# Hybrid attention and retention trunk on one core: lower parts of V, queries and keys deferred by a tick, retention's norm a round later, norms and output scales one operation per round

## The chip, the core and the metric

The kernel runs on one core of a Trainium2 chip. A core has five engines with instruction queues of their own: TensorE (PE) does matmuls into PSUM, VectorE (DVE), ScalarE (ACT) and GpSimd (POOL) do elementwise work, and SyncE (SP) issues nearly all DMA transfers of this kernel. Each engine works through its queue in order, and waits at an instruction whose inputs or buffers are not ready. The metric is the time of one execution on the device in microseconds. The kernel before takes 2124.11 us, the median of 3 runs (2123.64 to 2125.86).

## What is computed

A trunk of two layers over 2048 tokens of width 1024. Each layer normalizes its input, projects it to eight sections of 512 columns, sends four through chunked attention (8 heads of 64) and three through chunkwise retention (4 heads of 128) with gates for both, and projects back with a residual. Cut to what matters:

```python
def hybrid_layer(x, norm_gain, w_in, w_out, rel_bias, cos, sin):
    hn = rms_norm(x, norm_gain)
    aq, ak, av, ag, rq, rk, rv, rg = jnp.split(hn @ w_in, cuts, axis=-1)
    ya = chunked_rel_attention(aq, ak, av, rel_bias)      # own chunk of 64 and 8 before
    yr = chunkwise_retention(rq, rk, rv, cos, sin)        # rotary q and k, decayed state, rms_norm per head
    y = jnp.concatenate([ya * jax.nn.silu(ag), yr * jax.nn.silu(rg)], axis=-1)
    return x + y @ w_out

def reference(x, positions, norm_gain, w_in, w_out, rel_bias, final_gain):
    cos, sin = rotary_tables(positions, RET_HEAD_DIM)
    for layer in range(DEPTH):
        x = hybrid_layer(x, ...)
    return rms_norm(x, final_gain)
```

Inputs and output are f32. The kernel computes each f32 product as three f16 products: each operand is held as an upper f16 part and a lower part (what the upper leaves over), and high x high, high x low and low x high are summed in PSUM.

## The kernel before

**Tiles and stages.** The tokens are 16 tiles of 128, four of them a block n (0 to 3). The columns are worked off in four groups s (0 to 3), of two attention heads and one retention head. A *stage* is (layer l, group s, block n): `dense_T` makes q, k and the two rotary sections, transposed (four groups of 24 matmuls with 512 columns), `dense_V` makes the attention's v, retention's v and both gates (four tiles, 24 matmuls each), and `attention` with `retention` inside works through the block's eight units of (tile, head) and four retention tiles. The attention of a stage runs one dense generator later, beside the next stage's matmuls. After the four groups, `wout` multiplies the gated output y with w_out, adds the residual and makes the next layer's normalized input (`residual`) or the output (`final`).

**What sets the order.** Everything is written as Python generators that `run` (L1113) interleaves. A round is: one step of the dense generator (a third, 8 matmuls); then `tick` (L613); then one step of the attention generator; then `pull` of some background steps (weight preparation, input norms, rotary tables), so many that the pushed steps are used up in the rounds left. The order of emission is the order in each engine's queue.

```python
def later(k, fn):
    deferred.append([k, fn])          # run by the k-th tick from now

def run(gen, att, thirds):
    for _ in gen:
        tick()
        ... next(att[0], att) ...
        ... pull(min(-(-todo // max(left, 1)), todo)) ...
```

A `later(1, ...)` made in a dense step is therefore run by the tick of the same round, after the older deferred steps that are due in it; one made in an attention or a background step is run in the next round.

**Evacuation of PSUM.** In `dense_T`, `evacuate` copies q (L637) and k (L647) to f16 on ACT; DVE takes the lower part from the same PSUM buffer and the copy (L638, L648), and SP spreads the halves over partitions. The rotary sections are copied to `raw`, swapped by DMA, turned with the tables by POOL (L668 to L670) and split (L673, L676, L679). In `dense_V` ACT makes the upper part of v, the gate's tanh and the upper part of retention's v (L757 to L759), and DVE makes the lower parts and the gate (L760, L762, L764).

**Retention.** For each tile, r1 holds the scores; three deferred steps mask them (L867), make dT's upper (L852) and lower part (L856). r2, from the same PSUM pool `psR` of four buffers (shared with the attention's output o and with the sums ms of weight preparation), holds the output in its first 128 columns and the state's increment in the next. Deferred steps follow: at 1 the state is added up (L888) and ACT squares the output into the SBUF tile `yr` (L909, one buffer) with a sum per row; at 2 the new state's upper part (L852) and the root (DVE L901, POOL L902); at 3 its lower part (L856) and the scaled, gated output (DVE L905), stored to `y_d` by SP (L907); at 4 the state is decayed (ACT L896).

**Norms and tables in the background.** Blocks 1, 2 and 3 need their input norms while group 0 runs: `norm` squares a tile with a row sum (ACT L206), takes the root (DVE L210, POOL L212), multiplies by root and gain (DVE L229), splits into halves (ACT L242, DVE L243) and transposes them by SP DMA into hTh and hTl (L250, L251). `norms_from_input` (L1127) interleaves the tiles of a block; block 1's are the list of steps at L1301, and blocks 2 and 3 are pushed at L1325 with 21 steps, followed by the rotary `tables` of the next block (DVE L93 to L124, stores L129 to L132) with 19 steps.

**Output projection.** `wout` (L1032) runs 6 rounds per tile. For the tile two ahead it loads y, squares it and scales (`y_scale`: ACT L938, DVE), splits it a round later (`y_split`: ACT L245, DVE L246), and turns it by SP transposes (`y_turn`) in round 0. The residual sum is L1069; `residual` then puts the next layer's norm steps at 2 to 8 rounds on, `final` the output's.

Of the kernel before, what the change touches and what calls it, by code (L numbers as in the profile page):

```python
# [18 lines left out]
P = 128  # L19
# [8 lines left out]
def hybrid_trunk(ctx: ExitStack, tc: tile.TileContext, x, pos, gain, gcol, w_in, w_out, rel, fgain,  # L28
# [174 lines left out]
    def rms(xt, m, e, nm, junk):  # L203

        ss = b2.tile([P, 1], F32, tag="ss", name=f"ss{nm}", bufs=4)
        act.activation(junk, xt, AF.Square, accum_out=ss)  # L206
        return rms_of(ss, m, e, nm)

    def rms_of(ss, m, e, nm):
        dve.tensor_scalar(ss, ss, m, e, op0=ALU.mult, op1=ALU.add)  # L210
# [10 lines left out]
    def norm(l, t, xt, rows=None):  # L221

        n, a = divmod(t, 4)
        hT_of(l, n)
        hh, hl = (h_[:, :, a * P:(a + 1) * P] for h_ in hT[l, n])
        nm = f"n{l}_{t}"
        rs = rms(xt.rearrange("p (k c) -> p k c", c=P), gains[l].m, gains[l].e, nm, hh)
        yield
        dve.scalar_tensor_tensor(out=xt, in0=xt, scalar=rs[:, 0:1], in1=gains[l].b, op0=ALU.mult, op1=ALU.mult)  # L229
        yield  # L230
        rw = split_rows(xt, nm, rows)
        yield
        transpose_rows(rw, hh, hl)
        yield

    def split_rows(xt, nm, rows=None, s_=None):

        if rows is None:
            rows = (b2.tile([P, 1280], F16, tag="sc", name=f"rh{nm}")[:, 0:D],
                    b2.tile([P, 1280], F16, tag="pq", name=f"rl{nm}")[:, 0:D])  # L240
        if s_ is None:
            act.activation(rows[0], xt, AF.Copy)  # L242
            dve.tensor_tensor(rows[1], xt, rows[0], op=ALU.subtract)  # L243
        else:
            act.activation(rows[0], xt, AF.Copy, scale=s_[:, 0:1])  # L245
            dve.scalar_tensor_tensor(out=rows[1], in0=xt, scalar=s_[:, 0:1], in1=rows[0], op0=ALU.mult, op1=ALU.subtract)  # L246
        return rows
# [374 lines left out]
    def dense_T(l, s, n, g, st):  # L622
# [9 lines left out]

        def evacuate(j, ps):
            if j == 0:
# [3 lines left out]
                dve.scalar_tensor_tensor(out=qq[:, 1, :], in0=ps, scalar=2.0 ** -16, in1=qq[:, 0, :], op0=ALU.mult,  # L638
                                         op1=ALU.subtract)
                for hx in range(2):  # L640
                    for half in range(2):
                        sp.dma_start(st.q[half * 64:half * 64 + 64, hx], qq[hx * 64:hx * 64 + 64])
            elif j == 1:
# [4 lines left out]
                dve.scalar_tensor_tensor(out=kl, in0=ps, scalar=2.0 ** -16, in1=kh, op0=ALU.mult, op1=ALU.subtract)  # L648
                sp.dma_start(st.k[0:64, 0, :], kh[0:64, :])
# [294 lines left out]
    def y_split(u):  # L944
        split_rows(u.y, u.nm, u.rows, u.sy)
# [496 lines left out]
```

## Time and profile before

| | us |
|---|---|
| median of 3 runs | 2124.11 |
| range of the runs | 2123.64 to 2125.86 |
| the profiled execution | 2123.54 |
| its span in the profile | 2121.8 |
| PE busy | 2018.0 (95%), 14014 matmuls |
| DVE busy | 1217.7 (57%) |
| ACT busy | 1161.2 (55%) |
| POOL busy | 687.7 (32%) |
| mean granted TensorE clock | 0.986 |

The page gives shares and slices of the span and the costliest groups of instructions. A group's row names line, engine, operation and tiles, then its busy time, the mean of one in ns, and the idle time before it with what ended it. Rows of waits read: engine, line that waited, what released it; then microseconds in total, times, and the longest. Rows of windows read: stretch and its length, then the busy time (and count) of PE, PEld (weight load), DVE, ACT and POOL, then the granted clock as a share of full speed, the busy share of the 16 DMA engines, and GB/s. Rows of a timeline read: start, duration, engine, line, operation, out<-in; in brackets the idle time before, with its releaser.

The execution falls into a prologue with stage (0,0,0) (0 to 75 us), the other stages of layer 0 (to 902), the first output projection (to 1102), the stages of layer 1 (to 1933) and the second output projection.

### The profile page before, as it was taken

The page shows a single profiled execution, that of the slowest core. Times are in us where ns is not written, and L with a number is a line of the kernel's source. Part 1 is how long each engine was busy: PE and PEld are TensorE (multiplying, and loading weights), DVE is VectorE, ACT ScalarE, POOL GpSimd, SP SyncE. Part 2 cuts the span into 40 slices and gives each one's busy share as a digit, 9 for nine tenths or more (in the row PEclk, how much of TensorE's full clock was granted, in tenths as well). Part 3 has the DMA queues.
Part 4 walks back from the last instruction along what each step waited for, and adds up shares of the span by engine and source line. Part 5 has one row for each costly group of instructions (what it writes and reads, how often), then busy time and mean ns, then how long its engine had stood idle before and what let it go on. Part 6 is the DMA issues. An engine that isn't in the chain of part 4 may idle for free. (4 is left out here: it accounts for less than half of the span.)

```text
span 2121.8 us, 39588 instructions
## 1 busy us (share of the span) xinstructions
PE 2018.0 (95%) x14014; PEld 1054.6 (50%) x14014; DVE 1217.7 (57%) x3839; ACT 1161.2 (55%) x2522; POOL 687.7 (32%) x701
## 2 busy tenths in 40 slices
PE   6788999999999999988999999999999999999998
PEld 4344455554455555444444555555545545554443
DVE  7677656555655555566653556555655565556543
ACT  7455665556655654555444546555665565556432
POOL 1233343443334334421002443434334433343200
PEclk9999999999999999999999999999999999999999
DMA  8757774558655764689865556555685566548874
GB/s 246 177 118 148 153 161 106 112 110 185 152 115 110 160 157 101 134 185 246 232 176 116 120 104 141 121 127 101 142 192 122 100 142 159 123 103 177 213 204 119
DMA packets 645702, 313.64 MB, mean 148 GB/s; under 512 B 459232, under 2 KB 602080, under 8 KB 645504
## 3 DMA queue, kind: packets, MB, share of 16 engines
q1 hardware_dynamic: 645504, 311.12, 65.4%
q8 instruction: 109, 1.79, 0.3%
q14 instruction: 89, 0.73, 0.1%
HBM read 123.26 MB, written 41.98 MB: 78 GB/s over the span
## 5 line engine op out<-in xcount | busy, mean ns | idle before, releaser
L803 POOL TENSOR_TENSOR pq<-sc,pq 128x640 f16<-128x640 f32 (+4 forms) x256 | 319.5, 1248 | 1037.1 <-ACT pq L802 622.9
L800 ACT ACTIVATE sc<-sc,mq,cT 128x640 f32<-128x640 f32 (+4 forms) x256 | 218.3, 853 | 359.6 <-DVE mq L799 241.6
L749 PE MATMUL dV<-wlV,hTh 128*128 128x512 f16 x1024 | 391.9, 383 | 5.4 <-DVE wlV L347 5.4
L749 PE MATMUL dV<-whV,hTh 128*128 128x512 f16 x1024 | 392.1, 383 | 4.6 <-DVE gt L764 3.7
L749 PE MATMUL dV<-whV,hTl 128*128 128x512 f16 x1024 | 391.8, 383 | 0.0
L729 PE MATMUL dT<-hTh,whT 128*128 128x512 f16 x1008 | 383.9, 381 | 6.2 <-DMA hTh<-hTl 6.2
L729 PE MATMUL dT<-hTl,whT 128*128 128x512 f16 x1008 | 383.5, 380 | 3.0 <-DMA hTl<-hTl 3.0
L729 PE MATMUL dT<-hTh,wlT 128*128 128x512 f16 x1008 | 383.5, 380 | 0.0
L749 PEld LDWEIGHTS <-hTh 128*128 128x128 f16 x2048 | 199.3, 99 | 224.8 <-issue 9.0
L729 PEld LDWEIGHTS <-whT 128*128 128x128 f16 x2016 | 194.9, 98 | 225.7 <-issue 11.5
L797 DVE CUSTOM_DVE_ANT_0 sc<-S,bias 128x640 f32<-128x640 f32 (+4 forms) x256 | 188.7, 737 | 145.6 <-PE S L794 144.7
L1066 PE MATMUL dO<-whO,yhy 128*128 128x512 f16 x512 | 194.7, 380 | 2.2 <-DVE hTl L1069 1.2
L1066 PE MATMUL dO<-whO,yly 128*128 128x512 f16 x512 | 194.7, 380 | 2.2 <-DMA yly<-rly 2.2
L1066 PE MATMUL dO<-wlO,yhy 128*128 128x512 f16 x512 | 194.8, 380 | 0.0
L802 ACT ACTIVATE pq<-sc 128x640 f16<-128x640 f32 (+4 forms) x256 | 171.5, 670 | 8.1
L760 DVE SCALAR_TENSOR_TENSOR v<-dV,v 128x128 f16<-128x128 f32 x128 | 37.2, 291 | 214.1 <-ACT rv L759 213.2
L749 PEld LDWEIGHTS <-hTl 128*128 128x128 f16 x1024 | 100.8, 98 | 116.3 <-issue 11.4
L1066 PEld LDWEIGHTS <-yhy 128*128 128x128 f16 x1024 | 99.9, 98 | 117.9 <-issue 4.7
L729 PEld LDWEIGHTS <-wlT 128*128 128x128 f16 x1008 | 98.9, 98 | 105.2 <-issue 2.3
L793 PE MATMUL S<-k,q 128*128 128x128 f16 (+3 forms) x592 | 143.4, 268 | 7.3 <-DVE mq L797 4.4
L813 PE MATMUL o<-v,pT 128*128 128x65 f16 x1120 | 130.6, 194 | 12.5 <-DMA pT<-pq 12.5
L814 PE MATMUL o<-v,pT 128*128 128x64 f16 x1120 | 130.8, 195 | 0.0
(350 smaller groups left out, 3561.1 us busy)
## 6 DMA issues: line engine op xcount, KB each, us to landing
q<-qq SPq DMA_DIRECT2D x128, 128.0 KB, 2.5
yyy<-y_d SPq DMA_DIRECT2D x32, 512.0 KB, 4.4
stT<-in_w_in_dram SPq DMA_DIRECT2D x27, 512.0 KB, 5.0
stV<-in_w_in_dram SPq DMA_DIRECT2D x26, 512.0 KB, 4.7
k<-kk SPq DMA_DIRECT2D x128, 64.0 KB, 2.1
swp<-rot SPq DMA_DIRECT2D x64, 128.0 KB, 2.6
tabc<-tab SPq DMA_DIRECT2D x32, 256.0 KB, 2.9
tabs<-tab SPq DMA_DIRECT2D x32, 256.0 KB, 2.9
```

The lines of the kernel that those rows point to most:

```text
L729: pe.matmul(ps, w_[:, j, kt, :], h_[:, kt, :], start=(m == 0), stop=(m == 23))
L749: pe.matmul(ps, h_[:, kt, a * P:(a + 1) * P], w_[:, kt, :], start=(m == 0), stop=(m == 23))
L760: dve.scalar_tensor_tensor(out=st.v[:, a, :, 65:129], in0=pv_, scalar=2.0 ** -16, in1=vh_, op0=ALU.mult, op1=ALU.subtract)
L793: pe.matmul(o, st.q[:, hx, 0, cs], k_, start=True, stop=False)
L797: dve.tensor_tensor_reduce(out=v, in0=S[:, 0:w], in1=g.bias[hx][:, 640 - w:640], scale=1.0, scalar=-3.0e38, op0=ALU.add, op1=ALU.max, accu ...
L800: act.activation(v, v, AF.Exp, bias=m[:, 0:1], scale=g.c[:, 0:1])
L802: act.activation(pq[:, 0:w], v, AF.Copy)
L803: pool.tensor_tensor(pq[:, w:2 * w], v, pq[:, 0:w], op=ALU.subtract)
L813: pe.matmul(o[:, 0:65], u.p[:, b, :], v_[:, 0:65], start=(b == 0), stop=False)
L814: pe.matmul(o[:, 0:64], u.p[:, b, :], v_[:, 65:129], start=False, stop=False)
L1066: pe.matmul(ps, h_[:, kt, :], w_[:, kt, :], start=(m == 0), stop=(m == 23))
```

## The change

Five edits, which leave the arithmetic as it is (the squares of retention's output are written to another place, and only their sum is used):

1. In `dense_T` and `dense_V`, DVE's lower parts of q, k and v and its gate product, with the DMAs behind q and k, are put into `later(1, ...)`. Stage (0,0,0) keeps q and k as they were. The third part of the rotary queries goes from d + 5 to d + 6.
2. In `retention`, Square, root and output move from 1, 2, 3 to 2, 3, 4; the state's decay from 4 to 5. Square writes to the third 128 columns of r2 in PSUM instead of `yr`, which is now allocated at the output.
3. `norm` and `split_rows` are taken apart into `squares`, `rms_of`, `rows_hi`, `rows_lo` and `transpose_rows`. `norms_from_input` becomes a plan of 21 rounds with one operation per tile in each, and every round takes one step of the next block's tables, which were pushed behind it before. The list for block 1 is repacked.
4. In `wout_first` and `wout`, y's Square, scale, upper half, lower half and transposes each get a round.
5. `final` and `residual` take the root a round after the Square and the lower half a round after the upper.

The core of the diff (the lambdas' defaults and unchanged bodies cut):

```diff
+        def soon(fn):
+            if first:
+                fn()
+            else:
+                later(1, fn)
...
                 act.activation(qq[:, 0, :], ps, AF.Copy, scale=2.0 ** -16)
-                dve.scalar_tensor_tensor(out=qq[:, 1, :], in0=ps, scalar=2.0 ** -16, in1=qq[:, 0, :], ...)
+                soon(q_rest)
...
-                        later(d + 4 if first else d + 5, third)
+                        later(d + 4 if first else d + 6, third)
...
             act.activation(rv[:, 2], rv[:, 0], AF.Copy, scale=2.0 ** -11)
+            def rests(...):
+                dve ... st.v lower part; dve ... rv[:, 1]; dve ... gt
+            later(1, rests)
...
-                later(4, lambda ns=ns: act.activation(ns, ns, AF.Copy, ...))
+                later(5, lambda ns=ns: act.activation(ns, ns, AF.Copy, ...))
...
-            later(1, lambda r2=r2, ss=ss, y=y: act.activation(y, r2[:, 0:P], AF.Square, accum_out=ss))
-            later(2, root)
-            later(3, fin)
+            later(2, lambda r2=r2, ss=ss: act.activation(r2[:, 2 * P:3 * P], r2[:, 0:P], AF.Square, accum_out=ss))
+            later(3, root)
+            later(4, fin)
...
+        for fns in ((), (lambda: y_squares(u),), (lambda: y_scale(u, go),), (lambda: rows_hi(u.rows, u.y, u.sy),),
+                    (lambda: rows_lo(u.rows, u.y, u.sy), lambda: y_squares(v)), (lambda: y_turn(u), lambda: y_scale(v, go)),
+                    (lambda: rows_hi(v.rows, v.y, v.sy),), (lambda: rows_lo(v.rows, v.y, v.sy),)):
...
-            if (i == 0 and T + 1 < NT and (end or T + 2 < NT)) or (i == 5 and T + 3 == NT and not end):
-                y_turn(us[T + 1 if i == 0 else T + 2])
+            hurry = T + 3 == NT and not end
+            if i == 0 and 0 < T < NT - 1 and (end or T + 2 < NT):
+                rows_lo(us[T + 1].rows, us[T + 1].y, us[T + 1].sy)
+            if (i == 1 and T + 1 < NT and (end or T + 2 < NT)) or (i == 5 and hurry):
+                y_turn(us[T + 1 if i == 1 else T + 2])
...
-            if i == 3 and T + 2 < NT:
-                y_scale(l, us[T + 2], go)
-            if i == 4 and T + 2 < NT:
-                y_split(us[T + 2])
+                if i == 3 - hurry:
+                    y_squares(v)
+                if i == 4 - hurry:
+                    y_scale(v, go)
+                if i == 5 - hurry:
+                    rows_hi(v.rows, v.y, v.sy)
...
+        plan = {0: [lambda: load(0)]}
+        add = lambda r, fn, k: plan.setdefault(r, []).append(lambda: fn(k))
+        for k in range(4):
+            if k:
+                add(4 * k - 4, load, k)
+            for i, fn in enumerate((sq, root, mul, hi, lo, dma)):
+                add(3 + 4 * k + i, fn, k)
+        for r in range(21):
+            for fn in plan.get(r, ()):
+                fn()
+            next(tab, None)
+            yield
+        for _ in tab:
+            yield
...
-    push(rounds(["xhi4 xrs5", "xlo4 xmul5", "xdma4 xhi5 xrs6 bt", "xlo5 xmul6", "xdma5 xhi6 xrs7", "xlo6 xmul7 u",
-                 "xdma6 xhi7", "xlo7 u", "xdma7 u u bt", "u u bt", "u u", "u u bt"]), 12)
+    push(rounds(["xhi4 xrs5 xrs6", "xlo4 xmul5 xrs7", "xdma4 xhi5 xmul6 bt", "xlo5 xhi6 u", "xdma5 xlo6 xmul7", "xdma6 xhi7",
+                 "xlo7", "xdma7 u", "u u bt", "u u bt", "u u", "u u bt"]), 12)
...
-                    push(norms_from_input(range(4 * n + 4, 4 * n + 8), late[0:4] if n == 1 else None), 21)
-                    push(tables(n + 1, [xs0[n + 1][:, i * 256:(i + 1) * 256] for i in range(4)]), TAB_STEPS)
+                    push(norms_from_input(range(4 * n + 4, 4 * n + 8), late[0:4] if n == 1 else None,
+                                          tables(n + 1, [xs0[n + 1][:, i * 256:(i + 1) * 256] for i in range(4)])), 21)
```

180 lines of the change are left out of this document (95 added, 85 removed).

## The prediction

> **What bounds the kernel now.** I read the page first, its busy shares and slices, then a table of stages, then the waits of each engine in the stages that lose time.
>
> ```profile
> span 2121.8 us, 39588 instructions
> PE 2018.0 (95%) x14014; PEld 1054.6 (50%) x14014; DVE 1217.7 (57%) x3839; ACT 1161.2 (55%) x2522; POOL 687.7 (32%) x701
> PE   6788999999999999988999999999999999999998
> ```
>
> PE is busy for 95% of the span. The slices are 53 us each: PE falls below 9 in the first four (the prologue and the first stages), in two near 900-1000 us (the start of the first output projection) and in the last. The order of PE's own instructions is the same in both kernels, matmul for matmul, so the time changes only where PE's waits and its granted clock change. The edits move DVE, ACT, POOL and SP work about; they matter only where PE waits.
>
> A stage (layer l, group s, block n) is one dense_T and one dense_V, with the attention of the block before beside it. Equal stages hold equal PE work, so a stage that loses time can be set beside a twin that loses none. The columns are the busy time of PE, PEld, DVE, ACT and POOL with their counts, then the granted clock, the DMA share and GB/s.
>
> ```profile
> 75.55:141.01 65.46, 53.37 (x289) 25.57 (x290) 47.27 (x127) 33.40 (x70) 18.33 (x23) 0.89 0.55 119
> 141.01:206.91 65.90, 56.10 (x402) 29.46 (x400) 47.30 (x121) 36.80 (x76) 25.52 (x23) 0.92 0.77 159
> 206.91:265.45 58.54, 53.27 (x412) 28.60 (x410) 35.98 (x122) 38.30 (x82) 22.08 (x19) 1.00 0.70 149
> 1144.28:1191.85 47.57, 47.48 (x294) 23.88 (x293) 26.75 (x98) 27.35 (x67) 15.57 (x17) 1.00 0.42 100
> 1191.85:1243.85 52.00, 52.00 (x402) 28.26 (x400) 29.15 (x99) 29.05 (x66) 21.76 (x20) 1.00 0.55 114
> 475.90:536.46 60.56, 55.07 (x407) 28.62 (x405) 32.56 (x113) 40.43 (x92) 21.32 (x23) 0.97 0.83 187
> 689.69:745.67 55.98, 54.32 (x407) 28.87 (x405) 30.82 (x109) 34.11 (x79) 21.41 (x24) 0.97 0.69 155
> 1503.34:1565.12 61.78, 54.45 (x407) 29.16 (x405) 33.60 (x113) 40.66 (x92) 21.80 (x23) 0.97 0.84 187
> 1296.08:1350.88 54.80, 52.36 (x407) 28.23 (x405) 31.51 (x109) 33.80 (x78) 20.94 (x23) 1.00 0.74 157
> 902.39:1102.09 199.70, 186.67 (x1064) 90.90 (x1062) 121.72 (x299) 98.68 (x174) 22.78 (x29) 0.99 0.89 212
> 1933.02:2121.80 188.78, 178.22 (x1010) 85.48 (x1007) 95.95 (x240) 70.95 (x122) 25.10 (x31) 0.99 0.69 181
> ```
>
> Stages (0,0,1) and (0,0,2), rows 1 and 2, take 65.5 and 65.9 us; their twins in layer 1, rows 4 and 5, take 47.6 and 52.0. So 17.9 + 13.9 = 31.8 us are lost there. These are the stages with input norms and rotary tables in the background: DVE is busy 47.3 us in each, against 26.8 and 29.2 in the twins. Stages (0,2,0) and (1,2,0), rows 6 and 8, take 4.6 and 7.0 us more than (0,3,0) and (1,1,0) below them. The output projections are the last two rows. The other stages run at their twins' 52 us, with PE at 99% or more: nothing is to be won there, only lost.
>
> **The change part by part.**
>
> *Prologue.* The first dense_T of block 1 waits twice for transposes that SP issues too late:
>
> ```profile
> 69.39 1.26 SPq L250 DMA_TRANSPOSE hTh<-hTl  x1
> 74.14 1.24 SPq L251 DMA_TRANSPOSE hTl<-hTl  x1
> 75.55 0.59 PE L729 MATMUL dT<-hTh,whT 128*128 128x512 f16 x1 [6.18 <-DMA hTh<-hTl]
> 79.12 0.59 PE L729 MATMUL dT<-hTl,whT 128*128 128x512 f16 x1 [2.98 <-DMA hTl<-hTl]
> ```
>
> The list of steps is repacked: the last two tiles' transposes come about one place sooner, with fewer transfers ahead of them on SP. One SP transpose is 1.25 us. I take -1.4 us, one such place; bounds 0 and -3 (the whole second wait).
>
> *Norms and tables in (0,0,1) and (0,0,2).* Before, a generator step does a Square together with its root, or an ACT copy together with DVE's subtraction, three steps in a round; the norms are through after ten rounds and the table steps then come in clumps. After, each step does one operation per tile and one table step beside it. The work is the same; what goes is the standing in line:
>
> ```profile
> ACT sc L800 <- DVE mq L799: 17.9, 13, 3.2
> ...
> ACT yr L909 <- DVE state L888: 12.8, 6, 5.8
> ...
> DVE ssn L210 <- ACT hTh L206: 7.4, 4, 2.2
> ...
> PE r L848 <- DVE dT L856: 7.0, 4, 2.1
> ...
> PE S L793 <- DVE mq L797: 4.4, 1, 4.4
> PE r L848 <- ACT dT L852: 3.8, 1, 3.8
> ```
>
> (Waits between 79 and 207 us: total, count, longest.) PE waits for DVE and ACT results which are themselves behind the clumps. How much comes back? DVE sets it: 47.3 us of work cannot fit a 47.6 or 52 us stage without gaps. It is busy 72% of both stages now. At 72% nothing is won; at 90% each takes 52.6 us, -13 each. I take 82%, about the middle: 57.7 us each, so -8 and -8.
>
> Against this stands SP. The last tile of the norms is loaded and turned near the end of the stage now; by the order of instructions its two transposes are issued about 4 us of PE work (matmuls between them at full pace) ahead of the dense_T(0,0,2) that reads them, where it was 24; ahead of dense_T(0,0,3) it is about 7 instead of 30. Queued before them are table stores and pT transposes:
>
> ```profile
> 138.56 0.48 SPq L132 DMA_DIRECT2D tab<-xb  x1
> ...
> 143.91 0.59 SPq L132 DMA_DIRECT2D tab<-xb  x1
> ```
>
> ```profile
> hTl<-rln SPq DMA_TRANSPOSE x14, 3.5
> ```
>
> Eight stores (the first and the last of them, about 0.55 us each) are 4.4 us of SP, then 1.25 us each for two transposes and 3.5 us to landing: 10.4 us from start to end against 4 us of lead, so 6 at worst. Part of the queue will have drained: +5 for block 2, bounds 0 and +8; +1 for block 3, bounds 0 and +4. Net of this part -10, bounds -26 and +12.
>
> *Retention's Square, root and output a round later; Square writes to PSUM.* Before, Square comes in the round of the state update, waits on ACT for DVE's queue, and writes to the single buffer yr that a store must leave first:
>
> ```profile
> ACT yr L909 <- DVE state L888: 88.7, 78, 5.8
> ACT yr L909 <- DMA y_d<-yr: 59.5, 23, 6.2
> ```
>
> ```profile
> ACT yr L909 <- DMA y_d<-yr: 8.7, 2, 6.0
> ...
> PE r L848 <- ACT dT L852: 3.5, 1, 3.5
> ```
>
> (Two rows of the whole run, two of 1503 to 1566 us.) Behind Square on ACT stand the softmax copies and dT, for which PE waits. Both reasons go. In (0,2,0) and (1,2,0), where the transfers are thickest (0.83 and 0.84 DMA share), the excess of 4.6 + 7.0 = 11.6 us over the siblings is what these waits can have caused; I take half, -6, bounds 0 and -11. Elsewhere PE did not wait for them: 0. What is late next: r2's PSUM buffer is read one round longer. A round is 52.00/24 = 2.17 us. The pool has four buffers and comes round in six rounds, sooner where weight preparation takes one: in some 18 places of the order the lead between the output's read and PE's next write shrinks from three rounds to two, 6.5 to 4.3 us. I take 0, with an upper bound below.
>
> *Lower parts of V, q and k.* Each is deferred by one tick, but a tick follows in the same round: the DVE parts move only behind the other steps due in it.
>
> ```profile
> DVE v L760 <- ACT rv L759: 213.2, 111, 10.7
> DVE qq L638 <- ACT qq L637: 48.2, 28, 2.7
> PE dV L749 <- DVE gt L764: 3.7, 3, 1.6
> ```
>
> DVE's 213 us of waiting for ACT is time that DVE may use for the due steps first, so dT and sh come sooner, while the dense PSUM buffer comes free later by those steps. Two such buffers alternate, so a whole group of three rounds, 6.5 us, stands between; PE waited only 3.7 us in all. I take 0, bounds -4 and +4.
>
> *Output projections.* Square, scale, copy, subtraction and transposes of each y tile go a round apart, the norm's root and lower half too.
>
> ```profile
> PE r L848 <- DVE dT L856: 5.4, 4, 2.5
> PE o L813 <- DMA pT<-pq: 3.1, 5, 1.0
> PE dO L1066 <- DMA yly<-rly: 2.2, 1, 2.2
> ```
>
> (902 to 1103 us.) PE is idle 199.70 - 186.67 = 13.0 us there; in the page's slices the dip lies at its start, where the last attention units still run. The 5.4 us behind DVE should shrink, as in the first stages; but y's transposes are issued a round later (2.17 us), against a landing that was late once already, by 2.2. I take -3, bounds -8 and +5; for the second projection, whose 10.6 us of idle are mostly its end, -1, bounds -3 and +2.
>
> **Sum:** -1.4 - 10 - 6 + 0 - 3 - 1 = -21.4 us. From the profiled execution (2123.54 us; span 2121.8 and 1.7 around it) that is 2102.1; the median of the runs is 0.57 higher, so 2102.7, say 2103.
>
> The clock has a part in this. In (0,0,1) idle is 12.1 us of the 17.9 lost; the other 5.9 are the same matmuls at a granted clock of 0.89. I count both as returning in proportion. The Trainium skill (TensorE: Matmul & The Clock Gate, Part 1) says that the array falls to half clock only after about 3.4 us of idleness and needs about as long to recover. By that rule the many waits of 1 to 2 us cost idle time alone, and removing them gives back no clock: two thirds of the -16, or 5 us less gain, 2108. The row with 0.89 and two waits over 3.4 us in two stages leans a little against it.
>
> **The rivals.**
>
> 1. *Late transposes take the gain.* The order speaks for it (4 us of lead against 10), the load (0.55 and 0.77 DMA share in these stages) does not. With +8 and +4 at the two block starts, and the first projection at +3 for its y tiles: -1.4 - 4 - 6 + 3 - 1 = -9.4, or 2114; with the second projection at its +2 also and (0,2,0), (1,2,0) at half, 2120. Chance 0.18.
>
> 2. *Slower: the r2 buffer.* If the output's read comes later than two rounds, PE's next write in that buffer waits, in each of the 18 places, and those stages ran without waits before. It decides at a DVE that is 4.3 us behind; the row of L888 above shows the update in the same round up to 5.8 us late. At that longest, 5.8 - 4.3 = 1.5 us a place, it is 18 x 1.5 = +27: 2130. Against it: 88.7/78 = 1.1 us is the mean, and Square and its waits no longer stand ahead. Chance 0.15.
>
> 3. *The change does not relieve DVE.* DVE's work itself is stretched by POOL's, and spreading the table steps over all rounds makes more of them meet POOL's.
>
> ```profile
> 134.90 1.07 DVE L820 TENSOR_TENSOR rl<-rl,kaV 128x1 f32<-128x1 f32 x1
> 140.42 0.16 DVE L820 TENSOR_TENSOR rl<-rl,kaV 128x1 f32<-128x1 f32 x1
> 134.80 1.16 POOL L803 TENSOR_TENSOR pq<-sc,pq 128x512 f16<-128x512 f32 x1 [5.17 <-ACT pq L802]
> ```
>
> One column took 1.07 us and ended with POOL's instruction, against 0.16 alone. Then the stages stay at 65 us, their -16 is 0, and the sum is -1.4 + 6 - 6 - 3 - 1 = -5.4: 2119. The Trainium skill (SBUF — State Buffer, Who interferes with whom) has this as a rule: a DVE instruction with two SBUF inputs and a GpSimd instruction that reads SBUF share a port, held for the whole instruction, and the later one blocks. The three rows agree with it. Chance 0.11, half of it within 0.2%.
>
> 4. *More comes back.* DVE at 90% and the transposes in time (-26), with -9 at the s=2 starts and -3 in the projections: 2124 - 1.4 - 26 - 9 - 3 = 2085 at the far end, 2092 at its middle. Chance 0.10.
>
> **How the numbers follow.** The forecast, 2103 with its own range of 2095 to 2112, has 0.46. A measurement of this kernel can tell about 0.2%, 4.2 us, from no change: faster is below 2119.9, slower above 2128.4. Faster: 0.46 + 0.10 + 0.14 of the first rival + 0.05 of the third = 0.75. Same: 0.04 + 0.05 + 0.02 of the second = 0.11. Slower: 0.13 of the second and 0.01 of the third = 0.14. The range 2090 to 2127 leaves out about a tenth on each side.
>
> **What would show it.** In the profile after: stages (0,0,1) and (0,0,2) near 57 to 58 us with DVE near 82% and the clock nearer 1; a new wait of dT on hTl or hTh near 140 and near 200 us, of 5 and 1 us; no wait of the Square on state or on y_d; (0,2,0) and (1,2,0) near 57 to 58 us; the first projection near 197. I am wrong if DVE stays near 72% in the first stages, if the new waits for transposes exceed 8 us, or if r, o or ms matmuls in stages that ran at 52 us now wait for DVE's L905 output.

## The result and the profile after

The changed kernel takes 2115.01 us, the median of 5 runs (2111.82 to 2117.65), against 2123.64 (2120.36 to 2125.86) before: a ratio of 0.9959, 95% interval 0.9944 to 0.9974. It is faster by 8.6 us, where 21 were forecast. Its profiled execution is the slowest of the five (2117.65 us, span 2115.9), so the stages below add up to a gain of 5.9.

The head of the page after:

```profile
span 2115.9 us, 39456 instructions
...
PE 2010.4 (95%) x14014; PEld 1052.1 (50%) x14014; DVE 1253.8 (59%) x3839; ACT 1139.1 (54%) x2522; POOL 679.5 (32%) x701
```

The stages after, in the order of the rows shown of before ((0,0,1) to (0,0,3), then (0,2,0), (0,3,0), (1,2,0), (1,1,0), and the two projections); columns as there:

```profile
76.35:142.41 66.06, 52.44 (x290) 25.00 (x290) 44.28 (x119) 33.40 (x70) 19.74 (x23) 0.88 0.64 138
142.41:209.01 66.60, 56.12 (x399) 28.95 (x399) 46.94 (x121) 37.45 (x80) 24.81 (x24) 0.94 0.73 150
209.01:268.74 59.73, 55.47 (x409) 29.39 (x410) 34.42 (x122) 34.70 (x76) 20.42 (x19) 0.95 0.64 138
477.05:536.36 59.31, 53.05 (x408) 28.38 (x405) 33.23 (x113) 39.83 (x91) 21.08 (x23) 0.99 0.91 199
690.16:744.35 54.19, 52.37 (x407) 28.22 (x404) 34.59 (x109) 33.63 (x79) 21.21 (x24) 1.00 0.74 160
1500.61:1562.46 61.85, 54.63 (x407) 28.94 (x405) 32.63 (x113) 40.19 (x93) 21.44 (x23) 0.95 0.89 192
1292.59:1348.15 55.56, 52.36 (x407) 28.21 (x405) 34.37 (x109) 33.57 (x79) 21.83 (x24) 1.00 0.76 156
900.93:1099.57 198.64, 186.37 (x1065) 90.96 (x1063) 121.63 (x299) 98.24 (x175) 24.87 (x28) 0.99 0.89 214
1929.53:2115.90 186.37, 177.75 (x1010) 85.25 (x1007) 98.42 (x240) 70.16 (x123) 25.31 (x31) 0.99 0.73 184
```

(0,0,1) and (0,0,2), where most of the gain was to be, are 0.6 and 0.7 us longer, and (0,0,3) is 1.2 longer. (0,2,0) gains 1.2, (1,2,0) nothing, the projections 1.1 and 2.4. What is left of the 5.9 us came from places for which the forecast had nothing, such as (0,3,0) with 1.8.

PE's waits from 76 to 209 us, the first two rows of stages (total, count, longest), and the place of the longest that lies inside them, first on PE, then on DVE, then on POOL (a wait of 7.8 us, left out of the list, is the one that ends where the first stage begins):

```profile
PE r L853 <- DVE dT L861: 11.5, 4, 5.3
...
PE dV L750 <- DVE gt L768: 3.4, 2, 2.1
...
PE dT L730 <- DMA hTl<-rln: 0.9, 1, 0.9
```

```profile
123.20 0.29 PE L853 MATMUL r<-rv,dT 128*128 128x128 f16 x1 [5.30 <-DVE dT L861]
```

```profile
117.84 2.24 DVE L1168 SCALAR_TENSOR_TENSOR hTl<-hTl,rsn,gb 128x1024 f32<-128x1024 f32 x1
120.00 1.35 DVE L115 TENSOR_SCALAR xb<-xb 128x256 f32<-128x256 f32 x1
121.39 1.30 DVE L116 TENSOR_SCALAR xb<-xb 128x256 f32<-128x256 f32 x1
122.61 0.34 DVE L910 SCALAR_TENSOR_TENSOR yr<-r,rss,gt 128x128 f32<-128x128 f32 x1
122.87 0.27 DVE L861 SCALAR_TENSOR_TENSOR dT<-dT,r 128x128 f16<-128x128 f16 x1
```

```profile
117.74 1.26 POOL L670 TENSOR_TENSOR raw<-raw,tabc 128x512 f32<-128x512 f32 x1
118.96 2.24 POOL L671 TENSOR_TENSOR swp<-swp,tabs 128x512 f32<-128x512 f32 x1
121.28 1.26 POOL L672 TENSOR_TENSOR raw<-raw,swp 128x512 f32<-128x512 f32 x1
```

One round's background is a norm step and a table step on DVE, the multiplication of L1168 and the pair of L115 and L116: 4.9 us, beside POOL's turn, in a round of 2.2 us. The next round's dT, 0.27 us of work, stands behind them, and PE waits 5.3 us for it. The next longest wait for dT, 3.8 us up to 187.7, stands behind a table step alone, two instructions of 1.43 and 1.24 us, again beside POOL's turn. The clumps did not go; each round has a small one now.

### The profile page after: what moved, and what is told of

Read it like the earlier page. It is cut to its first block, busy times and chain, and to the rows that moved or that the text cites. A ratio compares the mean times of both kernels' runs of the same rounds, so it can differ in the third digit from the quotient of the medians.

```text
span 2115.9 us, 39456 instructions
## 1 busy us (share of the span) xinstructions
PE 2010.4 (95%) x14014; PEld 1052.1 (50%) x14014; DVE 1253.8 (59%) x3839; ACT 1139.1 (54%) x2522; POOL 679.5 (32%) x701
## 4 chain that ended last, share of the span: by engine, by line
PE 47%; DMA 3%; ACT 2%; DVE 2%; issue 1%; POOL 1%; SPq 1%; POOLq 0%; DVEq 0%; ACTq 0%
PE dT L730 14%; PE dV L750 14%; PE dO L1090 12%; DMA pT<-pq 2%; PE r L853 2%; PE S L799 1%; PE S L798 1%; PE o L818 1%; PE o L819 1%; PE o L820 1%; DVE sc L802 1%; ACT sc L805 0%; ACT pq L807 0%; DMA yhy<-rhy 0%; DMA bias<-toep 0%
## 5 line engine op out<-in xcount | busy, mean ns | idle before, releaser
L730 PE MATMUL dT<-hTh,whT 128*128 128x512 f16 x1008 | 386.0, 383 | 11.9 <-DVE rv L766 7.8
L1090 PE MATMUL dO<-whO,yhy 128*128 128x512 f16 x512 | 194.8, 381 | 1.9 <-DMA yhy<-rhy 1.9
L818 PEld LDWEIGHTS <-pT 128*128 128x128 f16 x1120 | 105.7, 97 | 51.0 <-DMA pT<-pq 21.5
```

The costliest lines, as they stand in the source:

```text
L730: pe.matmul(ps, w_[:, j, kt, :], h_[:, kt, :], start=(m == 0), stop=(m == 23))
L818: pe.matmul(o[:, 0:65], u.p[:, b, :], v_[:, 0:65], start=(b == 0), stop=False)
L1090: pe.matmul(ps, h_[:, kt, :], w_[:, kt, :], start=(m == 0), stop=(m == 23))
```

## The experiments

Four kernels first take one edit alone on the kernel before, then four join them, then eight look for the causes. One sentence of the description above is too strong: the order of emission is only nearly the order in each queue. With V's lower parts alone, whose lines touch DVE only, some 30 of SP's 1402 transfers, most of them stores of yr, stand at other places in SP's queue, so a kernel with one edit differs from the kernel before in a few places more than its lines. In the table, each time stands against the median of the kernel before in the same set of runs (2123.64 us for the whole change; 2119.81, 2121.37, 2119.35 and 2120.36 us for the four sets after it). Kernels of different sets are compared by what they gain there. A stage named below is read from one profiled execution of each kernel.

| kernel | median us | against before | ratio, 95% interval |
|---|---|---|---|
| whole change | 2115.01 | -8.6 | 0.9959 (0.9944 to 0.9974) |
| edit 3 alone (norms, tables) | 2126.46 | +6.7 | 1.0034 (1.0022 to 1.0046) |
| edit 2 alone (retention) | 2138.51 | +18.7 | 1.0089 (1.0075 to 1.0103) |
| edit 1 alone (lower parts) | 2111.17 | -8.6 | 0.9963 (0.9950 to 0.9977) |
| edits 4 and 5 alone (projections) | 2108.45 | -11.4 | 0.9951 (0.9938 to 0.9963) |
| edits 1, 4, 5 | 2105.49 | -15.9 | 0.9927 (0.9915 to 0.9940) |
| all but edit 3 | 2109.49 | -11.9 | 0.9940 (0.9926 to 0.9954) |
| all but edit 2 | 2107.76 | -13.6 | 0.9933 (0.9919 to 0.9948) |
| edits 1, 4, 5, Square in PSUM | 2104.48 | -16.9 | 0.9921 (0.9908 to 0.9933) |
| whole, no POOL turn in two stages | 2107.34 | -12.0 | 0.9936 (0.9921 to 0.9951) |
| whole, less table arithmetic | 2110.28 | -9.1 | 0.9961 (0.9949 to 0.9973) |
| tiles three rounds apart | 2107.35 | -12.0 | 0.9941 (0.9927 to 0.9954) |
| edit 2 and V's lower parts | 2118.64 | -0.7 | 0.9997 (0.9987 to 1.0007) |
| whole, table steps moved | 2102.90 | -17.5 | 0.9920 (0.9905 to 0.9935) |
| three rounds apart, table steps moved | 2094.50 | -25.9 | 0.9881 (0.9864 to 0.9897) |
| whole, no sines | 2109.51 | -10.9 | 0.9950 (0.9933 to 0.9966) |
| V's lower parts alone | 2117.06 | -3.3 | 0.9985 (0.9974 to 0.9996) |

### The edits one by one

**Edit 3 alone.** The kernel before with the new `norms_from_input`, its pushes and the repacked list; all else as before.

```diff
-                    push(norms_from_input(range(4 * n + 4, 4 * n + 8), late[0:4] if n == 1 else None), 21)
-                    push(tables(n + 1, ...), TAB_STEPS)
+                    push(norms_from_input(range(4 * n + 4, 4 * n + 8), late[0:4] if n == 1 else None,
+                                          tables(n + 1, ...)), 21)
```

> The kernel before with the third edit alone: norms and tables one operation per round, and the repacked list for block 1. Theory A (what I predicted: clumps made the queue, spreading them frees DVE): stages (0,0,1) and (0,0,2) take about 58 us each instead of 65.5 and 65.9, and the time is 8 to 12 us below before. Rival B (DVE is bound by its work, stretched beside POOL's rotary turns; the wait for dT only moves): both stages stay within 2 us of 65.5, and the time is within 3 us of before.

It costs 6.7 us. (0,0,1) takes 65.6 us (65.5 before); (0,0,2) goes from 65.9 to 69.5:

```profile
76.57:142.20 65.63, 53.15 (x289) 25.08 (x290) 42.61 (x118) 34.74 (x72) 17.98 (x23) 0.88 0.63 138
142.20:211.71 69.51, 57.78 (x399) 30.01 (x399) 45.22 (x121) 37.41 (x78) 26.24 (x24) 0.90 0.72 144
```

DVE is busy 65% of both. Theory A has fallen; B had the first stage, but neither the 69.5 nor that the edit would cost time. At the end of (0,0,2) PE now waits 3.7 us for the last tile's transpose.

**Edit 2 alone.** Retention's Square, root and output at 2, 3 and 4, the decay at 5.

```diff
-            later(1, lambda r2=r2, ss=ss, y=y: act.activation(y, r2[:, 0:P], AF.Square, accum_out=ss))
-            later(2, root)
-            later(3, fin)
+            later(2, lambda r2=r2, ss=ss: act.activation(r2[:, 2 * P:3 * P], r2[:, 0:P], AF.Square, accum_out=ss))
+            later(3, root)
+            later(4, fin)
```

> The kernel before with the second edit alone: retention's Square, root and output a round later, Square into PSUM. Theory A (the Square's waits on ACT held back dT): stages (0,2,0) and (1,2,0) lose 3 us each, the time is 5 to 7 us below before. Rival B (behind the Square stand other waits of ACT, for the DMAs of weights and of bias tiles): these two stages change by under 1.5 us each, the time is 0 to 3 us below before.

Neither: it costs 18.7 us. (0,2,0) and (1,2,0) change by under 1 us, as B had it. The loss is elsewhere: (0,1,1), (0,2,1), (1,0,1), (1,1,1) and (1,2,1) take 0.9 to 2.4 us more, and in each of them PE has one new wait of about 1 us for the output; (0,0,3), (0,3,3) and (1,3,3) take 4.4, 2.5 and 2.9 us more, with other waits. One of the five places, on DVE and then on PE (in this kernel V's lower parts are L786 to L790, the root L928, the output L933):

```profile
590.99 0.29 DVE L786 SCALAR_TENSOR_TENSOR v<-dV,v 128x128 f16<-128x128 f32 x1 [0.62 <-ACT rv L783]
591.20 0.34 DVE L788 SCALAR_TENSOR_TENSOR rv<-dV,urvV,rv 128x128 f16<-128x128 f32 x1
591.46 0.41 DVE L790 SCALAR_TENSOR_TENSOR gt<-gt,dV 128x256 f32<-128x256 f32 x1
...
591.99 0.27 DVE L928 TENSOR_SCALAR rss<-rss,raV,reV 128x1 f32<-128x1 f32 x1
592.92 0.35 DVE L933 SCALAR_TENSOR_TENSOR yr<-r,rss,gt 128x128 f32<-128x128 f32 x1 [0.66 <-POOL rss L929]
```

```profile
593.32 0.27 PE L876 MATMUL r<-rv,dT 128*128 128x128 f16 x2 [0.95 <-DVE yr L933]
```

PE waits for the output to leave r2. In DVE's queue the output stands behind V's lower parts, which wait for ACT, and behind the root, for whose part on POOL it waits another 0.66 us. These five waits are 4.8 us together; for the rest of the 18.7 no single cause is shown.

**Edit 1 alone.** The lower parts of q, k and v and the gate product in `later(1, ...)`.

```diff
+                soon(q_rest)
...
+                soon(k_rest)
...
-                        later(d + 4 if first else d + 5, third)
+                        later(d + 4 if first else d + 6, third)
...
+            later(1, rests)
```

> The kernel before with the first edit alone: lower parts of q, k, v and the gate product deferred by a tick. Theory A (as predicted: nothing): within 2 us of before. Rival B (the gains at the starts of the groups s=1 and s=3 in the changed kernel, some 5 us in all, come from DVE no longer waiting for ACT there): 3 to 6 us below before, in the stages (0,1,0), (0,3,0) and (1,3,0).

8.6 us faster: rival B, and more than it said. (0,1,0), (0,3,0) and (1,3,0) gain 2.1, 3.2 and 4.6 us. In the last two, PE's wait for the weights' lower part (wlV, made by DVE) falls from 1.18 and 1.19 us to 0.33 each, and the low clock behind it is gone (0.80 and 0.78 from 716 to 724 us before, 1.00 in this kernel). The waits of DVE at V's lower part for ACT fell from 213.2 us to 130.4 (60 times), and PE's waits for pT from 12.5 to 5.7 us; its waits for dT did not fall (15.8 us before, 20.7 here).

**Edits 4 and 5 alone.** The functions `wout_first`, `wout`, `residual` and `final` of the change.

```diff
-                y_turn(us[T + 1 if i == 0 else T + 2])
+                y_turn(us[T + 1 if i == 1 else T + 2])
...
+        at(3, root)
...
+            at(6, lower)
```

> The kernel before with the fourth and fifth edit alone: y's steps in the output projections and the root and lower half of norms each in a round of their own. Theory A (predicted 3 + 1): 3 to 5 us below before, most of it in the first projection. Rival B (y's later transposes take it back in the first projection, and the second, whose rounds the final norm shares, gains): 2 to 4 us below before, at least two thirds of it in the second projection.

11.4 us faster, the largest gain of the four and more than either theory. In its profile the first projection takes 194.8 us, 4.9 less, and the wait for dT there has gone from 5.4 us to 0.2; the second gains 2.1. Rival B's share between them was wrong. Another 2.1 us each come from (0,3,3) and (1,3,3), the stages beside which `wout_first` runs.

### The edits together

**Edits 1, 4 and 5.**

> The kernel before with the first edit (lower parts) and the fourth and fifth (projections), without retention's later rounds and without the norms and tables. Theory C (the edits that won alone, 8.6 and 11.4 us, act in different places and add up): 18 to 21 us below before. Rival D (both shorten the same queue on DVE at the ends of the groups, so the second brings little): 11 to 14 us below before.

15.9 us, between the two theories: the two gains add up only in part.

**All but edit 3.**

> All edits except the third (norms, tables and the repacked list). The third alone cost 6.7 us, most of it a wait for the last transposes ahead of stage (0,0,3). Theory C (it costs the same inside the whole change): 5 to 8 us faster than the whole change, so 14 to 17 us below before, stage (0,0,2) about 5 us shorter than in the whole change. Rival D (with DVE relieved by the other edits the norms' order costs nothing): within 3 us of the whole change, 6 to 11 us below before.

11.9 us below before, between the two theories. Against the whole change the ratios are 0.9940 and 0.9959 and their intervals overlap, so the cost of edit 3 inside the change, some 3 to 4 us, is likely and not certain.

**All but edit 2.**

> All edits except the second (retention's later rounds, Square in PSUM). The second alone cost 18.7 us. Theory C (a cost of the r2 buffer held a round longer, wherever DVE is late): 8 to 19 us faster than the whole change, so 17 to 28 us below before. Rival D (the cost of the second edit came from its lower parts of v standing in front of the late output in DVE's queue, which the first edit puts behind it): within 3 us of the whole change, 6 to 11 us below before.

13.6 us below before, between the two theories. 0.9933 against 0.9959, intervals that touch: edit 2 costs about 5 us inside the change. Beside edits 1, 4 and 5, in one set of runs, it costs 4.0 (2109.49 against 2105.49). So it is neither 18.7 nor nothing.

**Edits 1, 4 and 5 with Square in PSUM.** The one part of edit 2 that takes a wait away without a later round:

```diff
-            y = b1.tile([P, P], F32, tag="yr", name=f"yr{nm}")
...
-            later(1, lambda r2=r2, ss=ss, y=y: act.activation(y, r2[:, 0:P], AF.Square, accum_out=ss))
+            later(1, lambda r2=r2, ss=ss: act.activation(r2[:, 2 * P:3 * P], r2[:, 0:P], AF.Square, accum_out=ss))
```

> As the kernel with the first, fourth and fifth edit, and retention's Square written to PSUM in its old round 1 (the output tile yr allocated at the output), root and output in their old rounds 2 and 3. It takes the Square's wait for the store of yr away without holding r2 longer. Theory A (that wait held back dT in the stages with thick transfers): 2 to 4 us below the same kernel without it, in the stages (0,2,0) and (1,2,0). Rival B (ACT waits for weight and bias transfers there anyway): within 1.5 us of the same kernel without it.

2104.48 against 2105.49 without it: rival B, within noise. Why the wait was worth nothing is seen in the whole change, where it is gone too. ACT and then POOL in (1,2,0) after:

```profile
1557.81 1.06 ACT L309 ACTIVATE stO1m<-stO1m 128x1024 f32<-128x1024 f32 x1 [1.84 <-DMA stO1m<-in_w_out_dram]
...
1560.73 0.83 ACT L581 ACTIVATE bias<-bias,ciT 128x640 f32<-128x640 f32 x1 [0.65 <-POOL bias L580]
1561.47 0.26 ACT L857 ACTIVATE dT<-r 128x128 f16<-128x128 f32 x1
```

```profile
1560.35 0.15 POOL L579 MEMSET bias<- 64x64 f32 x1 [4.43 <-DMA bias<-toep]
```

Behind the Square stood a piece of w_out that was still being loaded, and a bias tile whose transfer POOL waits 4.4 us for. dT is last again, and PE waits for it as before (4.5 us; 3.5 before).

### What holds the first stages

**No POOL turn.** The whole change, with this in `turn`:

```diff
+                        if (l, s, n) in ((0, 0, 1), (0, 0, 2)):
+                            return
```

> The whole change with POOL's rotary turn (three f32 instructions on each of the rotary queries and keys) left out in the stages (0,0,1) and (0,0,2), so these rotary values are not turned. Theory L (DVE is stretched beside POOL's turns, which is why spreading DVE's steps freed nothing): DVE's busy time falls by 4 us or more in each of the two stages, the waits of PE for dT of 5.3 and 3.8 us shrink, and the two stages together are 6 to 12 us shorter. Rival W (what holds the stages is the number of DVE steps and the order of its queue): they are under 4 us shorter together.

```profile
77.57:140.04 62.47, 52.12 (x290) 24.98 (x290) 38.84 (x118) 33.52 (x70) 11.41 (x17) 0.90 0.67 146
140.04:204.11 64.07, 54.59 (x398) 28.41 (x399) 42.89 (x121) 36.85 (x79) 15.74 (x17) 0.96 0.75 155
```

No DVE instruction is taken out, yet DVE's busy time falls by 5.4 and 4.1 us, and the stages by 3.6 and 2.5. PE's longest wait for dT falls from 5.3 us to 2.6, and the three instructions that stood ahead of it, 4.9 us in the whole change, take 1.9:

```profile
118.39 1.28 DVE L1170 SCALAR_TENSOR_TENSOR hTl<-hTl,rsn,gb 128x1024 f32<-128x1024 f32 x1
119.59 0.29 DVE L115 TENSOR_SCALAR xb<-xb 128x256 f32<-128x256 f32 x1
119.91 0.29 DVE L116 TENSOR_SCALAR xb<-xb 128x256 f32<-128x256 f32 x1
```

So the stretch beside POOL is real, and 3.0 of those 4.9 us are stretch. Together the two stages gain 6.1 us, the low end of theory L; that is what the turn costs with all that hangs on it, so the stretch alone is worth at most as much.

**Less table arithmetic.** The whole change, with 16 of DVE's 21 instructions left out in the tables of blocks 2 and 3.

```diff
+        dv = dve if n < 2 else Nothing()
...
-            dve.scalar_tensor_tensor(out=dst, in0=kk, scalar=-c, in1=dst, op0=ALU.mult, op1=ALU.add)
+            dv.scalar_tensor_tensor(out=dst, in0=kk, scalar=-c, in1=dst, op0=ALU.mult, op1=ALU.add)
```

> The whole change with most of DVE's arithmetic of the rotary tables of blocks 2 and 3 left out (16 of 21 instructions of 256 columns in each, so those tables are wrong); loads, sines and stores stay. Theory W (DVE's amount of work bounds the stages (0,0,1) and (0,0,2)): they get 8 us or more shorter together, about the DVE time taken out. Theory L (the stretch beside POOL bounds them): 3 to 6 us, since fewer instructions meet POOL's. Rival S (late transposes and PSUM buffers bound them): under 3 us together, and the waits at the starts of blocks 2 and 3 stay.

```profile
76.09:141.91 65.82, 52.54 (x289) 25.11 (x290) 38.01 (x103) 33.63 (x70) 20.44 (x23) 0.88 0.64 138
141.91:207.24 65.33, 56.30 (x398) 29.47 (x399) 39.96 (x105) 36.75 (x78) 23.06 (x23) 0.95 0.71 153
```

6.3 and 7.0 us of DVE's work are gone, and the stages are 0.2 and 1.3 us shorter. The amount of DVE's work does not bound these stages: theory W falls. The time is the one of rival S, and the waits at the block starts stay as it said. The longest wait, which S does not name, stays too, at 5.7 us: the pair L115 and L116 was among the five instructions kept, and dT still stands behind it and the norm step.

**No sines.** `AF.Sin` replaced by `AF.Copy` for blocks 2 and 3, so that ACT needs no other function table.

```diff
-        act.activation(r, ang, AF.Sin)
+        act.activation(r, ang, AF.Sin if n < 2 else AF.Copy)
```

> The whole change with the sines of the tables of blocks 2 and 3 replaced by copies (those tables are wrong), so that ACT loads no other function table there. Theory T (two loads of 1.28 us in front of V's evacuation make PE wait for the gate, 2.05 and 1.32 us): these two waits go and what follows them, 4 to 7 us below the whole change. Rival N (PE's wait only moves to the next late result): under 2.5 us.

PE's wait for the gate goes, as theory T said, but 2.3 us is all (rival N), and not certain, since the two intervals overlap. At the block starts PE now waits longer for the transposes (hTl 3.2 us, 1.6 in the whole change). Its waits from 74 to 260 us:

```profile
PE r L854 <- DVE dT L862: 10.4, 4, 5.3
...
PE dT L731 <- DMA hTl<-rln: 3.2, 2, 2.4
...
PE dT L731 <- DMA hTh<-rhn: 3.1, 1, 3.1
```

**Tiles three rounds apart.** Edits 1, 4, 5 with Square in PSUM, and edit 3's plan with the list for block 1 as before and

```diff
-                add(4 * k - 4, load, k)
+                add(3 * k - 3, load, k)
...
-                add(3 + 4 * k + i, fn, k)
+                add(3 + 3 * k + i, fn, k)
```

> The kernel with the first, fourth and fifth edit and Square in PSUM in its old round, plus the third edit's plan with tiles three rounds apart instead of four, so the last transposes of a block are issued three rounds sooner, and the list for block 1 as before. Theory S (the third edit's loss is the late transposes at the block starts, 2.5 and 4.6 us, against gains of 1.9 and 3.9 us ahead of them): the block starts lose nothing, and the time is 3 to 6 us below the kernel without the third edit, about 2100. Rival D (tiles closer together clump again): no better than that kernel, 2104 to 2108.

2107.35, no better than without the plan: rival D's number. The late transposes are gone, as theory S had it, but another transfer stands in line. PE's wait, and SP's queue around the start of block 3 (at 207 us):

```profile
PE o L818 <- DMA pT<-pq: 5.9, 2, 3.1
```

```profile
198.05 1.28 SPq L237 DMA_TRANSPOSE hTl<-rln  x1
199.41 0.54 SPq L129 DMA_DIRECT2D tab<-xb  x1
...
203.83 0.59 SPq L132 DMA_DIRECT2D tab<-xb  x1
...
206.48 1.92 SPq L810 DMA_TRANSPOSE pT<-pq  x1
```

From the first of eight table stores to pT, with the loads of the tables and of a weight between, SP's queue takes 7 us. PE's waits for DVE are still there as well, 7.0 us for dT and 6.3 us for the softmax's maximum (mq), so D's reason is not excluded.

**Table steps moved.** The whole change, with the table steps two at a time in rounds in which no norm step uses DVE for a whole tile:

```diff
-            next(tab, None)
+            for _ in range(0 if r > 4 and r % 2 else 2):
+                next(tab, None)
```

> The whole change, with the table steps two at a time in the rounds in which no norm step uses DVE for a whole tile, none in the others; the table's stores then come in round 14 instead of 18. Theory S (a norm step and a table step in one round are more DVE than a round holds, and the eight stores stand in SP's queue in front of the block start): the wait for dT of 5.3 us and the block-start losses of 2.5 and 4.6 us halve, 4 to 8 us below the whole change. Rival N (the place of the steps does not matter, their meeting with POOL does): within 3 us of the whole change.

```profile
76.94:137.56 60.62, 51.89 (x289) 24.90 (x290) 42.85 (x117) 32.93 (x70) 20.05 (x23) 0.91 0.67 149
137.56:199.54 61.98, 54.47 (x398) 28.53 (x399) 44.78 (x123) 37.54 (x79) 24.21 (x24) 0.97 0.79 163
```

```profile
PE r L853 <- DVE dT L861: 4.2, 4, 2.3
```

2102.90, 17.5 us below before; its interval (0.9905 to 0.9935) lies clear of the whole change's. The two stages get 5.4 and 4.6 us shorter with the same work: theory S, in its first half. PE's waits for dT from 74 to 260 us go from 11.5 us to the 4.2 of the last row, and those for the gate, 3.4 us, are gone. The second half did not come: the waits for transposes at the block starts, 2.0 and 3.7 us, are 1.9 and 2.7, and 3.2 us of waits for pT are new. This is the line that the whole change lacked.

**Both.** The kernel with tiles three rounds apart, with the table steps through by round 12 (counted from 0):

```diff
+            for _ in range(2 if r < 5 else 3 if r % 3 == 0 else 0):
+                next(tab, None)
```

> The plan with tiles three rounds apart on the first, fourth and fifth edit with Square in PSUM in its old round, and the table steps all within the first 12 rounds, two or three at a time in rounds without a norm step on DVE. Theory S (with the transposes early, it was the table stores in SP's queue that made pT late by 2.8 and 3.1 us at the block starts): these two waits go, 4 to 7 us below the same kernel with one table step a round, about 2101. Rival N: within 3 us of that kernel, and other waits take their place.

2094.50, 25.9 us below before and the fastest of all. PE's waits for pT from 74 to 260 us went from 5.9 us to

```profile
PE o L818 <- DMA pT<-pq: 0.4, 2, 0.2
```

and the gain over its parent, 12.7 us by the two ratios, is nearly twice the upper end that theory S gave. The waits for pT are under half of it: those for dT, for mq (6.3 to 3.3 us) and for the gate (3.2 us, now none) fell as well.

### Retention and the lower parts

**Edit 2 with V's lower parts.** Edit 2, and of edit 1 the part below; q and k as before.

```diff
-            rests()
+            later(1, rests)
```

> The kernel before with the second edit (retention later) and, of the first, only the lower parts of v and the gate product deferred. The second edit alone cost 18.7 us; beside the first, fourth and fifth it cost 4.0. Theory D (in DVE's queue the lower parts of v, which wait for PE and ACT, stood in front of the late output): the cost shrinks to 0 to 6 us above before. Rival Q (the lower parts of q and k did it, or r2's buffer itself): 12 us or more above before.

0.7 us below before, where edit 2 alone was 18.7 above: theory D, and more than it said. No wait of PE for the output's L933 is left in its list.

**V's lower parts alone.** The same two lines on the kernel before.

> The kernel before with V's lower parts and the gate product alone deferred by a tick; q and k as before. Theory D (DVE stood at V's lower parts for ACT, 213 us in all, in front of steps that were ready): 6 to 9 us below before, all of what the first edit gave. Rival Q (q and k gave at least half): 1 to 4 us below before.

3.3 us below before (interval 0.9 to 5.5), so V's part gave less than half of the first edit's 8.6: rival Q. DVE's waits at V's lower part fell as far as with the whole first edit (129.6 us, 60 times), so they are not what the 8.6 measure; PE's wait for wlV in (0,3,0) and (1,3,0) stays at 1.19 us. V's part is worth about 19 us beside edit 2, and 3 without it.

## Why the prediction was wrong

The direction was right, the size 2.5 times too large, and the terms fell apart.

- *Norms and tables, -10: the step that failed.* I took "82%, about the middle" for DVE's busy share in the two stages, as if DVE's work were what fills them. It was 67% and 70% after, which was the first of the signs of being wrong, and taking out 13 us of that work gave 1.5. The stages, forecast 8 us shorter each, got 0.6 and 0.7 longer. What holds PE longest there is a late dT, behind whatever the round before put on DVE: 4.9 us for a norm step and a table step in one round, 3.0 of them stretch beside POOL's turn. The description of the change has it ("every round takes one step"), and I counted steps per stage where a round was the unit. With the same steps in other rounds (the kernel with table steps moved) the two stages take 8.8 us less than before, against the 10 that I had forecast net.
- *Late transposes, +5 and +1, the first rival.* In the profile after, PE waits about 2.0 and 3.7 us for them at the two block starts. The rival's time, 2114, is the one that came, but that is luck: its sum keeps the 16 us of the two stages and the 6 of retention, and neither came. With the transposes early (tiles three rounds apart) pT behind the table stores took their place in SP's queue.
- *Retention, -6 at the s = 2 stages.* -1.2 and 0. I named Square's two waits and not what stood behind them, the loads of w_out and bias. I halved the bound without a reason from the trace.
- *Retention's r2, 0, the second rival.* Edit 2 alone makes a cost real: +18.7, of which 4.8 us are waits for the buffer, in five places and not eighteen. Inside the change it costs 4 to 5, since the first edit takes V's lower parts out of the way. I had "a DVE that is 4.3 us behind" as the point from which it decides, and did not say that the first edit decides it.
- *Lower parts, 0.* -8.6 alone. I argued that PE waited only 3.7 us for the gate. The gain is elsewhere: V's part gives 3.3 of it, and the rest came with the lower parts of q and k and the later third part of the rotary queries, in part as PE's shorter wait for the weights' lower part in (0,3,0) and (1,3,0). My "dT and sh come sooner" is not what gave it: PE's waits for dT grew by 4.9 us in that kernel, and those for sh fell by 2.1. The whole of the 8.6 is not accounted for.
- *Projections, -3 and -1.* -11.4 alone by the median; -1.1 and -2.4 in the profile after. The sum had nothing for (0,3,3) and (1,3,3), where `wout_first` runs: 2.1 us each alone, 0.1 each in the whole change, since edit 1 alone makes these two stages 1.3 and 1.5 us longer. Beside edit 1 these edits give 7.3 instead of 11.4; the rest of the loss is not settled.
- *Prologue, -1.4.* +0.8. The seven profiled executions with the repacked list start block 1 at 74.2 to 77.7 us, the eleven without it at 74.5 to 76.8 (before at 75.6), so this stays open.
- *The lock, the third rival.* Its condition came true: the stages stay at 66.1 and 66.6 us. Without POOL's turn the same DVE instructions take 9.5 us less, and the stages at most 6.1 us less, so it was a large part and not the whole cause. That bears out the rule of the Trainium skill (SBUF — State Buffer, Who interferes with whom) for the multiplication of L1168, which has two inputs in SBUF (2.24 us beside POOL, 1.28 without). The pair L115 and L116 has one input, which the rule as I gave it does not cover, and was stretched more (1.35 and 1.30 us, 0.29 without).

The cost of the edits one by one is +5.4 (6.7 + 18.7 - 8.6 - 11.4), and -8.6 together: 14 us are interaction. Edit 2 beside V's lower parts saves 16 us (18.7 - 3.3 one by one, -0.7 together); against that, edits 1, 4 and 5 lose 4.1 us beside each other. A sum of terms that are each priced alone has no place for that.

## What to carry to other kernels

In a kernel whose queues are kept in step by rounds, price a background step by the round that it falls in, not by the stage, and by what the other engines do in that round: the late result is whatever stands behind the fullest round. Before a deferral is taken for harmless, look at what the deferred instruction will stand behind in its new round, and which instruction ahead of it waits for another engine. And where a wait is to go, find the next transfer or instruction in that queue first, because it may inherit the wait.

## What the runs showed of the hardware

The granted clock falls after waits of PE, and not after long ones alone. The profile after, in stretches of 4 us:

```profile
120.00:124.00 4.00, 0.80 (x5) 0.56 (x6) 3.93 (x9) 0.04 (x1) 2.46 (x2) 0.50 0.07 16
124.00:128.00 4.00, 4.00 (x25) 1.88 (x24) 2.24 (x6) 3.96 (x8) 0.91 (x1) 0.74 0.22 49
128.00:132.00 4.00, 3.06 (x15) 1.18 (x12) 0.00 (x0) 3.97 (x7) 0.00 (x0) 1.00 0.88 168
```

The 5.3 us wait (117.9 to 123.2) brings the clock to 0.50, and it is back at 1.00 only after 128; the wait of 2.05 us that begins at 131 leaves it at 1.00 in its stretch and in the next. That agrees with the Trainium skill (TensorE: Matmul & The Clock Gate, Part 1), by which the array slows after some 3.4 us of idleness. Other waits do not agree with it: in the same profile a wait of 1.90 us that ends at 999.2 is followed by 0.58 (1000 to 1004), and before, a wait of 2.78 us that ends at 185.5 by

```profile
184.00:188.00 4.00, 2.50 (x24) 1.71 (x25) 3.83 (x13) 3.57 (x9) 1.87 (x2) 0.74 0.90 208
188.00:192.00 4.00, 4.00 (x20) 1.78 (x18) 4.00 (x8) 1.01 (x3) 3.92 (x4) 0.84 0.54 111
```

So a wait of about 2 us can bring the clock down and can leave it; what decides is not shown here. That the trace of before leans against the rule, as the prediction had it, holds, and a short wait that is removed can give back clock too.
